# Two norm changes in a two-layer decoder on eight cores: squares folded on VectorE ahead of the sum matmul, and mixer norms moved ahead in program order

## The chip, the cores and the metric

One Trainium2 chip; the kernel runs on all 8 of its cores. Each core computes one prompt sequence of 2048 tokens and 16 sample sequences of 8 tokens; nothing is exchanged between cores. The metric is the device time of the slowest core, in microseconds (us). Some executions are slow: a die (cores 0 to 3 or 4 to 7) then shows a lower granted clock.

## The reference, cut to what matters

```python
def rmsnorm(x, g):
    y = x * rsqrt(mean(x * x, axis=-1) + EPS)
    return y * g

for i in range(2):                               # layers; D_MODEL 1024, D_FF 4096
    a = rmsnorm(h, norm_mix[i])                  # "mixer norm"
    u, bg, cg, v = split(a @ w_in[i])            # 4 x 512 columns
    y_pool = pool(u) * pool_scale[i]             # trailing-window means, then a 128x128 map per group
    y_conv = bg * conv3(cg * v)
    h = h + concat(y_pool, y_conv) @ w_out[i]
    m = rmsnorm(h, norm_mlp[i])
    h = h + relu(m @ w_up[i]) ** 2 @ w_down[i]
    gate = sigmoid(rmsnorm(h, norm_ple[i]) @ w_ple_gate[i])
    h = h + gate * (p[i] @ w_ple_proj[i])        # "gated stage"
return rmsnorm(h, norm_f), ...                   # "final norm", and the pool and conv states
```

There are seven norms over all tokens: three in each layer and the final one.

## The kernel before

The kernel holds h in SBUF with channels on partitions (8 blocks of 128) and tokens along the row, in five tiles of 512, 512, 512, 384 and 256 tokens. So a norm must sum squares across partitions. TensorE does that with an all-ones weight, once per block, adding up in PSUM:

```python
def norm(t, gbase, dst, dstB, halves=False):
    ...
        for hf in range(2):
            items = []
            for k in range(4 * hf, 4 * hf + 4):
                ...                                        # q: one of 4 square buffers
                P.op("act", ... activation(out=sq[:, q, 0:cn], in_=h[:, k, o:o + cn], func=AF.Square) ...)
                items.append((ones[:], sq[:, q, 0:cn], [onesB, sqB[q]]))
            ps = P.mm(items, cn, ps=ps, last=(hf == 1))    # 2 x 4 matmuls
        P.op("act", ... activation(out=rstd..., in_=ps..., func=AF.Ln, ...), kind="ln")
        P.op("act", ... activation(out=rstd..., in_=rstd..., func=AF.Exp, scale=-0.5), kind="ln")
        for k in range(KT):                                # 8 normalized blocks on VectorE
            P.op("dve", ... scalar_tensor_tensor(out=dst(k)..., in0=h[:, k, ...], scalar=gamma, in1=rstd...) ...)

def mixer_in(l, t, w):
    norm(t, V_NMIX + l * 8, ...)        # the norm of tile t stands right ahead of its matmuls
    ...                                 # 4 pool groups, then 4 conv groups
```

A list scheduler turns this program order into one fixed instruction stream per engine before the kernel is built. TensorE may draw operations from a window of 40 in program order.

Ln and Exp need one ScalarE table set (`kind="ln"`), the gated stage's Sigmoid another. Squares, copies and Relu run in either: of the 27 table loads in the trace before, 26 stand at the lines of Ln, Exp and Sigmoid, and one at a first Ln that the program issues at its start.

## Time and profile before

| | before |
|---|---|
| time, median of the first 5 runs | 1560.6 us |
| spans of the cores, profiled run | 1555.3 to 1558.5 us |
| matmuls that sum squares | 288 |
| ScalarE table loads | 27 |
| TensorE, VectorE, ScalarE busy | 98%, 57%, 34% |

The prediction below shows the page's lines and says how to read them. In all views PE is TensorE, PEld its weight loads, DVE VectorE, ACT ScalarE, POOL GpSimd and SP SyncE; L with a number is a line of that run's kernel.

### The profile page before, as it was taken

The numbers are of one execution on the slowest core, as the hardware profiler recorded it, in microseconds if no ns is written. First come the engines' busy times: TensorE is split into PE (matmuls) and PEld (weight loads), VectorE is DVE, ScalarE is ACT, GpSimd is POOL, SyncE is SP. The second block draws the span as 40 slices with busy tenths as digits, with TensorE's granted clock in tenths as the row PEclk, the third lists the DMA queues.
The fourth block names the chain that finished last, engine by engine and source line by source line (L and its number), as shares of the span: only waits on it lengthen the run. The fifth ranks groups of instructions, "written<-read, shape, count | busy, mean of one in ns | idle before, by whom it ended". The sixth has DMA issues, their size and how long they took to land.

```text
span 1558.5 us, 25041 instructions; the slowest of 8 cores (1555.3 to 1558.5 us)
## 1 busy us (share of the span) xinstructions
PE 1526.1 (98%) x8284; PEld 807.8 (52%) x8284; DVE 889.9 (57%) x1668; ACT 522.5 (34%) x1012; POOL 64.7 (4%) x122
## 2 busy tenths in 40 slices
PE   7999999999999999999989999999999999999997
PEld 4444565555555555454534446555555555554544
DVE  5758875444444444477677787744444444445778
ACT  4344453103103103335343444530230230233676
POOL 3000010000000000000000001000000000000000
PEclk9999999999999999999999999999999999999998
DMA  8900083421221221103230003722221221200024
GB/s 187 230 1 0 1 135 55 69 41 29 40 41 28 41 41 28 28 8 55 33 66 1 1 1 54 132 30 52 41 41 28 41 39 30 41 1 1 1 80 166
DMA packets 26062, 75.67 MB, mean 49 GB/s; under 512 B 2512, under 2 KB 7376, under 8 KB 25904
## 3 DMA queue, kind: packets, MB, share of 16 engines
q0 software_dynamic: 17600, 60.69, 22.8%
q1 hardware_dynamic: 8192, 13.31, 2.5%
q8 instruction: 71, 1.16, 0.3%
q14 instruction: 55, 0.45, 0.1%
q10 hardware_dynamic: 144, 0.05, 0.0%
HBM read 118.28 MB, written 10.10 MB: 82 GB/s over the span
## 4 chain that ended last, share of the span: by engine, by line
PE 91%; DVE 4%; DMA 2%; issue 1%; ACT 1%; POOL 0%; DVEq 0%; SPq 0%; ACTq 0%; POOLq 0%
PE ps L361 91%; DVE arena L576 2%; DMA poolw<-pool_w 1%; DVE h L720 1%; DVE arena L644 1%; DMA h<-x 1%; DVE h L576 0%; ACT sq L565 0%; DVE arena L652 0%; ACT arena L627 0%; ACT rstd L573 0%; ACT rstd L571 0%; POOL ring L529 0%; DVE arena L706 0%; DVE h L770 0%
## 5 line engine op out<-in xcount | busy, mean ns | idle before, releaser
L361 PE MATMUL ps<-arena,ring 128*128 128x512 bf16 (+2 forms) x7840 | 1464.9, 348 | 6.8 <-DVE arena L576 6.0
L361 PEld LDWEIGHTS ps<-arena,ring 128*128 128x128 bf16 x7840 | 767.0, 98 | 685.1 <-issue 19.3
L720 DVE TENSOR_TENSOR h<-h,ps 128x512 f32<-128x512 f32 (+2 forms) x400 | 241.6, 607 | 273.7 <-PE ps L361 273.3
L735 ACT ACTIVATE arena<-ps 128x512 f32<-128x512 f32 (+2 forms) x320 | 170.6, 533 | 640.5 <-PE ps L361 623.2
L736 DVE TENSOR_TENSOR arena<-arena 128x512 bf16<-128x512 f32 (+2 forms) x320 | 195.5, 612 | 268.1 <-ACT arena L735 267.9
L565 ACT ACTIVATE sq<-h 128x512 bf16<-128x512 f32 (+2 forms) x288 | 142.2, 546 | 133.3 <-PE ps L361 70.9
L576 DVE SCALAR_TENSOR_TENSOR arena<-h,vec,rstd 128x512 bf16<-128x512 f32 (+2 forms) x248 | 148.3, 654 | 26.7 <-ACT rstd L573 26.5
L361 PE MATMUL ps<-sq,ones 128*128 128x512 bf16 (+2 forms) x288 | 69.5, 351 | 11.1 <-ACT sq L565 10.1
L644 DVE TENSOR_TENSOR arena<-arena 128x526 f32<-128x526 f32 (+8 forms) x100 | 67.2, 672 | 6.9 <-ACT arena L627 4.3
L768 DVE TENSOR_TENSOR arena<-arena,ps 128x512 f32<-128x512 f32 (+2 forms) x80 | 47.4, 605 | 33.7 <-ACT arena L766 29.0
L706 DVE SCALAR_TENSOR_TENSOR arena<-arena,vec 128x512 f32<-128x512 f32 (+2 forms) x80 | 53.9, 676 | 19.5 <-ACT arena L702 15.9
L766 ACT ACTIVATE arena<-ps 128x512 f32<-128x512 f32 (+2 forms) x80 | 41.3, 532 | 49.9 <-PE ps L361 44.2
L361 PEld LDWEIGHTS ps<-sq,ones 128*128 128x128 bf16 x288 | 28.1, 98 | 43.1 <-issue 20.8
L770 DVE TENSOR_TENSOR h<-h,arena 128x512 f32<-128x512 f32 (+2 forms) x80 | 47.4, 610 | 4.6
L702 ACT ACTIVATE arena<-arena,vec 128x512 f32<-128x512 f32 (+2 forms) x40 | 30.1, 753 | 50.3 <-DVE arena L686 41.2
L627 ACT ACTIVATE arena<-ps 128x512 f32<-128x512 f32 (+2 forms) x48 | 22.7, 474 | 62.3 <-PE ps L361 51.0
L529 POOL DMA_DIRECT2D ring<-w_up x32 | 16.9, 530 | 615.8 <-PE ps L361 615.1
L686 DVE TENSOR_TENSOR arena<-arena,ps 128x512 f32<-128x512 f32 (+2 forms) x48 | 25.3, 530 | 15.9 <-PE ps L361 12.7
L681 ACT ACTIVATE arena<-ps 128x512 f32<-128x512 f32 (+2 forms) x48 | 22.3, 471 | 32.5 <-PE ps L361 28.9
L529 POOL DMA_DIRECT2D ring<-w_down x32 | 16.9, 529 | 324.0 <-PE ps L361 322.5
L664 ACT ACTIVATE arena<-ps,vec 128x512 bf16<-128x512 f32 (+2 forms) x40 | 24.8, 619 | 15.6 <-PE ps L361 15.6
L652 DVE SCALAR_TENSOR_TENSOR arena<-arena 128x512 bf16<-128x512 f32 (+2 forms) x48 | 25.7, 535 | 3.1 <-DVE carryE L631 0.4
(40 smaller groups left out, 230.3 us busy)
## 6 DMA issues: line engine op xcount, KB each, us to landing
ring<-w_up POOLq DMA_DIRECT2D x32, 512.0 KB, 6.3
ring<-w_down POOLq DMA_DIRECT2D x32, 512.0 KB, 6.5
ring<-w_in POOLq DMA_DIRECT2D x16, 512.0 KB, 9.5
y_t<-h SPq DMA_DIRECT2D x12, 512.0 KB, 2.8
h<-x POOLq DMA_DIRECT2D x4, 1024.0 KB, 29.2
ring<-w_out POOLq DMA_DIRECT2D x8, 512.0 KB, 25.5
ring<-w_gate POOLq DMA_DIRECT2D x8, 512.0 KB, 5.1
h<-x SPq DMA_DIRECT2D x4, 512.0 KB, 8.8
```

The lines of the kernel that those rows point to most:

```text
L361: return eng.matmul(self.psum[o.ps.bank][:, 0:o.width], lhsT=l, rhs=r, start=(o.first and j == 0), stop=(o.last and j == n - 1))
L529: o = P.dma("pool", lambda e, s=s, src=src: e.dma_start(out=ring[:, s, :], in_=src), 128 * 2048 * 4, f"ring{s}", writes=[ringB[s]], after= ...
L565: P.op("act", lambda e, q=q, k=k, o=o, cn=cn: e.activation(out=sq[:, q, 0:cn], in_=h[:, k, o:o + cn], func=AF.Square), c_act(cn), reads=[h ...
L576: P.op("dve", lambda e, n=n, k=k, o=o, c0=c0, cn=cn: e.scalar_tensor_tensor(out=dst(k)[:, c0:c0 + cn], in0=h[:, k, o:o + cn], scalar=vcol( ...
L644: P.op("dve", lambda e, to=to, src=src, v=v, sh=sh: e.tensor_tensor(out=af(to + v, ew - v), in0=af(src + v, ew - v), in1=af(src + v - sh, ...
L706: P.op("dve", lambda e, zo=zo, co=co, cwb=cwb, i=i: e.scalar_tensor_tensor(out=af(zo, zn), in0=af(co + i, zn), scalar=vcol(cwb + 4 * i), i ...
L720: P.op("dve", lambda e: e.tensor_tensor(out=h[:, c, toff:toff + tw], in0=h[:, c, toff:toff + tw], in1=ps.ap()[:, 0:tw], op=ALU.add), c_dve ...
L735: P.op("act", lambda e: e.activation(out=af(ro, tw), in_=ps.ap()[:, 0:tw], func=AF.Relu), c_act(tw), ps=[ps], writes=[rB])
L736: P.op("dve", lambda e: e.tensor_tensor(out=f_ap[t][c], in0=af(ro, tw), in1=af(ro, tw), op=ALU.mult), c_dve(tw), reads=[rB], writes=[fB[t] ...
L766: P.op("act", lambda e, ro=ro, p1=p1: e.activation(out=af(ro, tw), in_=p1.ap()[:, 0:tw], func=AF.Sigmoid), c_act(tw), ps=[p1], writes=[rB] ...
L768: P.op("dve", lambda e, ro=ro, p2=p2: e.tensor_tensor(out=af(ro, tw), in0=af(ro, tw), in1=p2.ap()[:, 0:tw], op=ALU.mult), c_dve(tw), ps=[p ...
L770: P.op("dve", lambda e, ro=ro, c=c: e.tensor_tensor(out=h[:, c, toff:toff + tw], in0=h[:, c, toff:toff + tw], in1=af(ro, tw), op=ALU.add), ...
```

## The change

The intent is to take norm sums off TensorE and to have the normalized blocks of the next mixer tile ready before TensorE needs them. The diff has five parts. The carry buffers' move into the arena (room for eight square blocks) is cut, as is the rest of the bookkeeping.

```diff
+        def first_norm():                       # layer 0, tile 0, in halves of 256; still 8 sum matmuls
+            ...
+                if i == 0:
+                    for o in P.ops[n0:]:
+                        o.lead = 4000.0         # schedule half 0 ahead of half 1's squares
+        def norm_stats(t, adds=True):
+            def add(a, b):                      # two blocks at once, bf16
+                P.op("dve", lambda e: e.tensor_tensor(out=sq[:, a:a + 2, 0:tw], in0=sq[:, a:a + 2, 0:tw], in1=sq[:, b:b + 2, 0:tw], op=ALU.add), ...)
+            for k in range(KT):
+                P.op("act", ... out=sq[:, k, 0:tw], in_=h[:, k, toff:toff + tw], func=AF.Square ...)
+                if adds and k % 4 == 3:
+                    add(k - 3, k - 1)
+            if adds:
+                add(0, 4)
+                P.op("dve", ... out=sq[:, 0, 0:tw], in0=sq[:, 0, 0:tw], in1=sq[:, 1, 0:tw], op=ALU.add ...)
+            ps = P.mm([(ones[:], sq[:, q, 0:tw], [onesB, sqB[q]]) for q in range(1 if adds else KT)], tw)
+            ...                                 # Ln, Exp
+        def norm_apply(t, n, gbase, dst, dstB): # the 8 normalizing instructions
 ...
         def mixer_in(l, t, w):
-            norm(t, V_NMIX + l * 8, lambda k: a[k][0], lambda k: aB[par][k], halves=(l == 0 and t == 0))
 ...                                             # pool half of tile t
+            if t + 1 < NT and (t > 0 or l == 0):
+                mix_apply(l, t + 1, norm_stats(t + 1))
 ...                                             # conv half of tile t
         def final(t):
-            norm(t, V_NF, lambda k: h[:, k, toff:toff + tw], lambda k: hB[k][t])
+            norm_apply(t, norm_stats(t, adds=t < 3), V_NF, lambda k: h[:, k, toff:toff + tw], lambda k: hB[k][t])
 ...
                 if l == DEPTH - 1:
                     final(t)
+                elif t == 1 or t == 3:          # in layer 0's gated stage: layer 1's first two mixer norms
+                    rs = norm_stats(t // 2)
+                elif t == 2 or t == 4:
+                    mix_apply(l + 1, t // 2 - 1, rs)
```

More of the change, by code (lines that the diff above doesn't have):

```diff
@@ L89, in __init__ @@
         self.fixed = None
+        self.lead = 0.0
 SEMLAT = 90.0
@@ L203, in schedule @@
                 a = min(a, ideal[o])
-            o.alap = a if o.fixed is None else -1e9 + o.fixed
+            o.alap = a - o.lead if o.fixed is None else -1e9 + o.fixed
         for o in ops:
@@ L409, in build @@
         arena = sb("arena", [128, AW], F32)
-        sq = sb("sq", [128, 4, 512], BF16)
+        sq = sb("sq", [128, KT, 512], BF16)
         rstd = sb("rstd", [128, 2, 512], F32)
@@ L415, in build @@
         invcnt = sb("invcnt", [128, 16], F32)
-        fix = sb("fix", [128, 16], F32)
-        carryE = sb("carryE", [128, 4, PB], F32)
-        carryC = sb("carryC", [128, 4, CB], F32)
         P.psum = [es.enter_context(nc.psum_tensor(f"ps{i}", [128, 512], F32)) for i in range(8)]
@@ L464, in build @@
         D_ = [take(256) for _ in range(2)]
+        CE_ = [take(PB) for _ in range(4)]
+        CC_ = [take(CB) for _ in range(4)]
         Z_ = [take(512), (M0 + 4 * W5, A.buf(M0 + 4 * W5, M0 + 4 * W5 + 512))]
@@ L469, in build @@
         SOUT = (T0, [A.buf(T0 + SO_P, T0 + SO_U), A.buf(T0 + SO_U, T0 + SO_C), A.buf(T0 + SO_C, T0 + SO)])
-        sqB = [Buf() for _ in range(4)]
+        SA = Arena()
+        sqB = [SA.buf(512 * k, 512 * k + 512) for k in range(KT)]
+        sqH = [[SA.buf(512 * k + 256 * i, 512 * k + 256 * i + 256) for i in range(2)] for k in range(KT)]
         rsB = [Buf() for _ in range(2)]
-        poolwB, vecB, onesB, invB, fixB = Buf(), Buf(), Buf(), Buf(), Buf()
-        ceB = [Buf() for _ in range(4)]
-        ccB = [Buf() for _ in range(4)]
+        poolwB, vecB, onesB, invB = Buf(), Buf(), Buf(), Buf()
+        fix, fixB = af(T0, 16), A.buf(T0, T0 + 16)
         ringB = [Buf() for _ in range(NSLOT)]
         halfB = [[Buf(), Buf()] for _ in range(NSLOT)]
-        st = dict(sq=0, rs=0, r=0, w=0)
+        st = dict(rs=0, r=0, w=0)
         def vcol(c):
@@ L551, in wk @@
             return ring[:, b.s, o:o + 128]
-        def norm(t, gbase, dst, dstB, halves=False):
-            toff, tw = TILES[t]
-            for i, (c0, cn) in enumerate([(0, 256), (256, 256)] if halves else [(0, tw)]):
-                hb = (lambda k: hH[k][i]) if halves else (lambda k: hB[k][t])
-                ab_ = (lambda k: aH[k][i]) if halves else dstB
-                o = toff + c0
-                ps = None
-                for hf in range(2):
-                    items = []
-                    for k in range(4 * hf, 4 * hf + 4):
-                        q = st["sq"]
-                        st["sq"] = (q + 1) % 4
-                        P.op("act", lambda e, q=q, k=k, o=o, cn=cn: e.activation(out=sq[:, q, 0:cn], in_=h[:, k, o:o + cn], func=AF.Square),
-                             c_act(cn), reads=[hb(k)], writes=[sqB[q]])
-                        items.append((ones[:], sq[:, q, 0:cn], [onesB, sqB[q]]))
-                    ps = P.mm(items, cn, ps=ps, last=(hf == 1))
-                n = st["rs"]
-                st["rs"] = 1 - n
-                P.op("act", lambda e, n=n, ps=ps, cn=cn: e.activation(out=rstd[:, n, 0:cn], in_=ps.ap()[:, 0:cn], func=AF.Ln, scale=1.0 / D, bias=EPS),
-                     c_act(cn), ps=[ps], writes=[rsB[n]], kind="ln")
-                P.op("act", lambda e, n=n, cn=cn: e.activation(out=rstd[:, n, 0:cn], in_=rstd[:, n, 0:cn], func=AF.Exp, scale=-0.5),
-                     c_act(cn), reads=[rsB[n]], writes=[rsB[n]], kind="ln")
-                for k in range(KT):
-                    P.op("dve", lambda e, n=n, k=k, o=o, c0=c0, cn=cn: e.scalar_tensor_tensor(
-                        out=dst(k)[:, c0:c0 + cn], in0=h[:, k, o:o + cn], scalar=vcol(gbase + k), in1=rstd[:, n, 0:cn],
-                        op0=ALU.mult, op1=ALU.mult), c_dve(cn, True), reads=[hb(k), rsB[n], vecB], writes=[ab_(k)])
@@ new lines, in rstd_of @@
+        def rstd_of(ps, n, tw):
+            P.op("act", lambda e: e.activation(out=rstd[:, n, 0:tw], in_=ps.ap()[:, 0:tw], func=AF.Ln, scale=1.0 / D, bias=EPS),
+                 c_act(tw), ps=[ps], writes=[rsB[n]], kind="ln")
+            P.op("act", lambda e: e.activation(out=rstd[:, n, 0:tw], in_=rstd[:, n, 0:tw], func=AF.Exp, scale=-0.5),
+                 c_act(tw), reads=[rsB[n]], writes=[rsB[n]], kind="ln")
+        def first_norm():
+            for i in range(2):
+                n0 = len(P.ops)
+                o = 256 * i
+                for k in range(KT):
+                    P.op("act", lambda e, k=k, o=o: e.activation(out=sq[:, k, o:o + 256], in_=h[:, k, o:o + 256], func=AF.Square),
+                         c_act(256), reads=[hH[k][i]], writes=[sqH[k][i]])
+                ps = P.mm([(ones[:], sq[:, k, o:o + 256], [onesB, sqH[k][i]]) for k in range(KT)], 256)
+                rstd_of(ps, i, 256)
+                for k in range(KT):
+                    P.op("dve", lambda e, i=i, k=k, o=o: e.scalar_tensor_tensor(
+                        out=ab(a_off[0] + k * 256, 512)[:, o:o + 256], in0=h[:, k, o:o + 256], scalar=vcol(V_NMIX + k), in1=rstd[:, i, 0:256],
+                        op0=ALU.mult, op1=ALU.mult), c_dve(256, True), reads=[hH[k][i], rsB[i], vecB], writes=[aH[k][i]])
+                if i == 0:
+                    for o in P.ops[n0:]:
+                        o.lead = 4000.0
@@ new lines, in norm_stats @@
+        def norm_stats(t, adds=True):
+            toff, tw = TILES[t]
+            def add(a, b):
+                P.op("dve", lambda e: e.tensor_tensor(out=sq[:, a:a + 2, 0:tw], in0=sq[:, a:a + 2, 0:tw], in1=sq[:, b:b + 2, 0:tw], op=ALU.add),
+                     75.0 + 1.042 * tw, reads=sqB[a:a + 2] + sqB[b:b + 2], writes=sqB[a:a + 2])
+            for k in range(KT):
+                P.op("act", lambda e, k=k: e.activation(out=sq[:, k, 0:tw], in_=h[:, k, toff:toff + tw], func=AF.Square),
+                     c_act(tw), reads=[hB[k][t]], writes=[sqB[k]])
+                if adds and k % 4 == 3:
+                    add(k - 3, k - 1)
+            if adds:
+                add(0, 4)
+                P.op("dve", lambda e: e.tensor_tensor(out=sq[:, 0, 0:tw], in0=sq[:, 0, 0:tw], in1=sq[:, 1, 0:tw], op=ALU.add),
+                     75.0 + 0.521 * tw, reads=sqB[0:2], writes=sqB[0:1])
+            ps = P.mm([(ones[:], sq[:, q, 0:tw], [onesB, sqB[q]]) for q in range(1 if adds else KT)], tw)
+            n = st["rs"]
+            st["rs"] = 1 - n
+            rstd_of(ps, n, tw)
+            return n
@@ new lines, in norm_apply, with norm @@
+        def norm_apply(t, n, gbase, dst, dstB):
+            toff, tw = TILES[t]
+            for k in range(KT):
+                P.op("dve", lambda e, k=k: e.scalar_tensor_tensor(out=dst(k), in0=h[:, k, toff:toff + tw], scalar=vcol(gbase + k),
+                                                                  in1=rstd[:, n, 0:tw], op0=ALU.mult, op1=ALU.mult),
+                     c_dve(tw, True), reads=[hB[k][t], rsB[n], vecB], writes=[dstB(k)])
+        def norm(t, gbase, dst, dstB):
+            norm_apply(t, norm_stats(t), gbase, dst, dstB)
@@ L580, in group, with mix_apply @@
+        def mix_apply(l, t, n):
+            par = t % 2
+            norm_apply(t, n, V_NMIX + l * 8, lambda k: ab(a_off[par] + k * 256, TILES[t][1]), lambda k: aB[par][k])
         def group(w, c, rhs, tw):
@@ L618, in mixer_in @@
                 else:
-                    P.op("dve", lambda e, eo=eo, g=g: e.tensor_copy(out=af(eo, PB), in_=carryE[:, g, :]), 80.0,
-                         reads=[ceB[g]], writes=[eB])
+                    P.op("dve", lambda e, eo=eo, g=g: e.tensor_copy(out=af(eo, PB), in_=af(CE_[g][0], PB)), 80.0,
+                         reads=[CE_[g][1]], writes=[eB])
                 if t == LT:
@@ L630, in mixer_in @@
                 if t < LT:
-                    P.op("dve", lambda e, eo=eo, g=g: e.tensor_copy(out=carryE[:, g, :], in_=af(eo + tw, PB)), 80.0,
-                         reads=[eB], writes=[ceB[g]])
+                    P.op("dve", lambda e, eo=eo, g=g: e.tensor_copy(out=af(CE_[g][0], PB), in_=af(eo + tw, PB)), 80.0,
+                         reads=[eB], writes=[CE_[g][1]])
                 else:
@@ L672, in mixer_in @@
                 else:
-                    P.op("dve", lambda e, co=co, j=j: e.tensor_copy(out=af(co, CB), in_=carryC[:, j, :]), 70.0,
-                         reads=[ccB[j]], writes=[cB])
+                    P.op("dve", lambda e, co=co, j=j: e.tensor_copy(out=af(co, CB), in_=af(CC_[j][0], CB)), 70.0,
+                         reads=[CC_[j][1]], writes=[cB])
                 if t == LT:
@@ L689, in mixer_in @@
                 if t < LT:
-                    P.op("dve", lambda e, co=co, j=j: e.tensor_copy(out=carryC[:, j, :], in_=af(co + tw, CB)), 70.0,
-                         reads=[cB], writes=[ccB[j]])
+                    P.op("dve", lambda e, co=co, j=j: e.tensor_copy(out=af(CC_[j][0], CB), in_=af(co + tw, CB)), 70.0,
+                         reads=[cB], writes=[CC_[j][1]])
                 else:
@@ L788, in build @@
                 w.setdefault(name, []).append(get())
+            if l == 0:
+                first_norm()
             mixer_in(l, 0, w)
```

## The prediction

> **What bounds the kernel now.** I read four views in this order: the list of cores (no die is slow: 1555.3 to 1558.5 us, clocks 0.991 to 0.994), the page, the groups by shape, and the table of stretches with the timeline around every place where TensorE stops.
>
> The page: TensorE is busy in 98% of the span, the chain that ended last lies on it for 91%, and the other engines are far from full on average. So time comes off only by taking matmuls away or by closing the gaps between them. The second row of groups is the target: 288 matmuls that only sum squares for the RMS norms (all-ones weights times the squared activations).
>
> ```profile
> PE 1526.1 (98%) x8284; PEld 807.8 (52%) x8284; DVE 889.9 (57%) x1668; ACT 522.5 (34%) x1012; POOL 64.7 (4%) x122
> ...
> PE 91%; DVE 4%; DMA 2%; issue 1%; ACT 1%; POOL 0%; DVEq 0%; SPq 0%; ACTq 0%; POOLq 0%
> ...
> L361 PE MATMUL ps<-sq,ones 128*128 128x512 bf16 (+2 forms) x288 | 69.5, 351 | 11.1 <-ACT sq L565 10.1
> ```
>
> Busy time is no cost here: 160 of these with 512 columns show a mean of 380 to 390 ns but overlap. The pace is what one more matmul costs, and the TensorE timeline gives it in unbroken runs:
>
> ```profile
> 38.45 13.98 PE L361 MATMUL ps<-arena,ring 128*128 128x512 bf16 x64
> ...
> 937.50 9.26 PE L361 MATMUL ps<-arena,ring 128*128 128x384 bf16 x56
> ...
> 1539.72 5.84 PE L361 MATMUL ps<-arena,ring 128*128 128x256 bf16 x52
> ```
>
> Taking off the last matmul's own 0.379, 0.324 and 0.269 us: 13.60/63 = 0.216, 8.94/55 = 0.1625, 5.57/51 = 0.109 us for 512, 384 and 256 columns. The span then splits like this. Real matmuls (4728, 1576 and 1576 of the three widths): 1021.2 + 256.1 + 172 = 1449 us. Norm sums after the first norm (160, 56, 56): 34.6 + 9.1 + 6.1 = 50. Start to the first real matmul: 19.8. Last matmul to the end: 9. Together 1528; the missing 30 us are stops and half-clock stretches.
>
> Where they lie (distances between matmul starts beyond the pace): 20 to 30 us 2.8, 53 to 62 us 4.0, 110 to 120 us 1.6, 170 to 210 us 3.2, 777 to 790 us 9.0, 870 to 890 us 2.0, 930 to 970 us 2.3, the last ten us of TensorE 3.3, and some 2 scattered. The table of stretches shows three of them; its columns are time and count on PE, PEld, DVE, ACT, POOL, then clock, DMA share, GB/s:
>
> ```profile
> 53.00:75.00 22.00, 20.57 (x85) 8.39 (x83) 18.98 (x37) 7.91 (x13) 0.00 (x0) 0.92 0.94 239
> ...
> 117.50:162.60 45.10, 43.62 (x202) 19.44 (x200) 38.12 (x73) 19.30 (x36) 0.00 (x0) 1.00 0.00 1
> ...
> 777.00:789.00 12.00, 6.48 (x20) 1.72 (x18) 6.25 (x12) 9.23 (x16) 1.06 (x2) 0.80 1.02 176
> 789.00:1000.00 211.00, 207.75 (x1102) 107.38 (x1102) 164.44 (x348) 93.54 (x196) 6.87 (x13) 1.00 0.18 30
> ```
>
> In 53 to 75, 85 matmuls at 0.216 would need 18.4 of the 22 us. In 777 to 789, the seam of the layers, only 20 matmuls run, and the clock falls. What TensorE waits for in a mixer is one normalized block at a time; VectorE makes one in (5.39 - 0.75)/7 = 0.66 us, TensorE uses it in 0.216. At the seam it is squares, the table load, Ln, Exp and then the blocks:
>
> ```profile
> 119.12 0.38 PE L361 MATMUL ps<-arena,ring 128*128 128x512 bf16 x1 [0.29 <-DVE arena L576]
> ...
> 781.21 1.28 ACT L571 ACT_TABLE_LOAD   x1 [0.60 <-PE ps L361]
> 782.51 0.60 ACT L571 ACTIVATE rstd<-ps 128x512 f32<-128x512 f32 x1
> ...
> 783.52 0.62 ACT L573 ACTIVATE rstd<-rstd 128x512 f32<-128x512 f32 x1
> ...
> 784.24 5.39 DVE L576 SCALAR_TENSOR_TENSOR arena<-h,vec,rstd 128x512 bf16<-128x512 f32 x8 [5.40 <-ACT rstd L573]
> ```
>
> **What the Trainium skill says.** "TensorE: Matmul & The Clock Gate", Wait — 56ns, not 53.3ns?: warm matmuls start N/2.4 GHz plus about 2.5 ns apart, 215.7 ns at 512 columns; the trace has 216, 162.5 and 109, so it agrees. The same page, What's actually happening: after an idle window of about 3.4 us the array runs at half clock. The trace agrees: mean clock 0.80 in the seam, 0.92 in 53 to 75. So closing a gap also takes back a slow stretch behind it. "VectorE: DVE Perf Modes", The perf-mode tier table: `tensor_tensor` on bf16 in SBUF makes two elements a cycle, on fp32 or from PSUM one. No all-bf16 add is in this trace, so this is untested here; the fp32 adds (0.69 us for 512 elements) agree with one. "Perfetto Trace Analysis", Optimizing Scalar/DVE Operations: each VectorE instruction on SBUF pays some 60 ns beyond its elements, about what the repeat distance of 0.61 us for 512 fp32 elements shows.
>
> **The change, part by part.**
>
> 1. Sums of squares. For 32 of the 35 tile norms, four VectorE adds fold the eight bf16 square blocks into one (three over two blocks, one over one), and one matmul replaces eight. Layer 0's first norm and the final norm of the last two tiles keep eight. The built instruction streams have 30, 14 and 20 such matmuls at 256, 384 and 512 columns, so 42, 42 and 140 go: 42 x 0.109 + 42 x 0.1625 + 140 x 0.216 = 4.6 + 6.8 + 30.2 = 41.6 us. All of it is TensorE time in stages that TensorE bounds, hence on the path.
>
> 2. VectorE's bill. At two elements a cycle the 1024-element add takes 0.53 + 0.08 = 0.62 us (estimate, rate from the DVE page, overhead from the trace), the last one 0.35: 2.2 us a 512-column norm, about 1.7 and 1.3 at 384 and 256. 20 + 6 + 6 norms: 44 + 10 + 8 = 62 us, so VectorE goes from 890 to about 950 of 1505 us, 63%. Beside TensorE in the MLP stages (VectorE 41 to 47% busy); not surely in the mixers. From 75 to 162.6 us VectorE does 26.6 + 38.1 = 64.7 us while TensorE issues 400 matmuls; a 512-column mixer tile (212 matmuls) is so 34.3 us of VectorE. After: 34.3 + 4.4 = 38.7 against 198 x 0.216 = 42.8 us of TensorE: 90%. Tight, but under.
>
> 3. Mixer norms earlier. The norm of tile t+1 now stands between the pool and conv halves of tile t, and layer 1's first two norms stand inside layer 0's gated stage (summed after tiles 1 and 3, applied after 2 and 4). So the blocks exist when TensorE arrives. In the built order 32 real matmuls for tile 1 follow tile 0's without a norm between, and at the seam the u-groups of layer 1 directly follow the last gate groups. The gated stage has room: VectorE 49.8 of 72 us, plus two norms (4.4 + 10.6) = 65. Two further table-load pairs there, 5.1 us of ScalarE, have room too (30 of 72).
> Expected: seam 9.0 to 0.5; 53 to 62 us 4.0 to 0.
>
> 4. Layer-0 start. Half 0's Ln and Exp no longer queue behind half 1's squares. Yet the chain of waits runs through the pool-weight load until 29.4 us, which nothing changes; only that 40 instead of 32 real matmuls precede it in the order. Gain at most 8 x 0.216 = 1.7 us.
>
> 5. Carry buffers and the small fix tile move into the arena to make room for eight square blocks: no cost that I find.
>
> Sum of stops afterwards: start 1.1; layer-0 mixers 4 (of 4.8 besides the closed gap: those at 110 and 170 to 210 shrink, VectorE at 90% makes others); seam 0.5; layer-1 mixers 3 (of 4.3); end 4.8, as VectorE has 6.6 us of adds more in a final stage where it was busy 62.7 of 80.5 us and TensorE now leaves 4.5 us earlier; scattered 2.5. That is 16 instead of 30. Time: 1560.6 - 41.6 - 14.5 = 1504 us, 3.6% less.
>
> **Rivals.** (a) VectorE becomes the mixers' bound. For it: 84% busy in 117 to 162 us already with stops, the adds are a dependent chain, and TensorE, which takes its instructions in order, now blocks at the sum matmul if the adds are late. Against it: 90% by count and TensorE has other groups ahead of each sum in the order. If so, 8 to 10 us more per layer: 1515 to 1525. (b) The adds run at one element a cycle: 1.15 instead of 0.62 us, 1.9 us a norm, a 512-column mixer tile then 42.5 of 42.8 us of VectorE; with stalls 1520 to 1530. The dense bf16 layout speaks against it. (c) Only the matmuls count, and the seam's wait moves elsewhere (ScalarE's extra tables delay the gated stage): 1560.6 - 41.6 + 2, about 1520. Layer 1's gated stage does the same table switches now without stopping TensorE before 1539 us, which speaks against it. (d) All stops of the mixers vanish and the end gains in full: about 1495.
>
> **Range and chances.** 1504, most likely with a tail to the slow side from (a) and (c); 1494 to 1518 should hold it 8 times in 10. A gain below 2% needs more than 1529, that is the whole closing of gaps lost and ten us of new stalls: 4%. Slower by over 2% would need VectorE to add some 70 us: 1%.
>
> **What would show it.** Step 1: 64 sum matmuls, none missing elsewhere. Step 2: 1024-element adds of about 0.7 us as the profile counts them (0.62 apart); 1.2 us would be rival (b). VectorE busy near 950. Step 3: no drop of the clock at the seam and no single matmuls waiting on the normalizing line after the pool-weight wait. Rival (a) would show TensorE idle before the sum matmuls or mixer matmuls, released by VectorE, over 8 us a layer. The prediction is wrong if TensorE's stops after the change do not fall below 20 us, or fall under 8.

## More of the kernel before

One more view is needed later: what happens once TensorE's last layer matmul has been issued. The table of stretches has time, then busy time and count on PE, PEld, DVE, ACT and POOL, then clock, DMA share and GB/s:

```profile
1538.00:1545.60 7.60, 7.51 (x66) 6.25 (x65) 7.49 (x18) 7.27 (x17) 0.00 (x0) 1.00 0.44 162
1545.60:1558.50 12.90, 1.80 (x8) 0.51 (x5) 9.45 (x22) 4.50 (x10) 0.00 (x0) 0.62 0.66 233
```

Three engines are full in the first row. In the second, TensorE has only norm sums left and VectorE works 9.45 of 12.9 us on 22 instructions. Then the last outputs are written.

The list scheduler lets TensorE draw operations from a window of 40 in program order.

Every other engine takes, of what is ready, the operation with the earliest latest-start time:

```python
pick = min((o for o in cs if ready[o] <= tau + 1.0), key=lambda o: (o.alap, o.i))
```

## The result, and the profile after

The changed kernel takes 1508.3 us (median of nine timed runs, 1508.1 over the fast ones) against 1561.0 us before: ratio 0.9666, 95% interval 0.9656 to 0.9676. Ratios here are the mean time of one kernel's fast runs over that of the other's in the same rounds, so they are not quite the ratio of the medians quoted. Executions in which one die ran at a lower clock are left out of the means. All runs gave correct results.

The page of the changed kernel, with the lines that answer to the prediction's first fence. The third is the group that sums squares:

```profile
PE 1477.9 (98%) x8062; PEld 784.6 (52%) x8062; DVE 934.1 (62%) x1796; ACT 536.9 (36%) x1020; POOL 64.7 (4%) x122
...
PE 93%; DVE 2%; DMA 2%; issue 1%; ACT 1%; POOL 0%; DVEq 0%; SPq 0%; ACTq 0%; POOLq 0%
...
L362 PE MATMUL ps<-sq,ones 128*128 128x256 bf16 (+2 forms) x64 | 19.0, 324 | 7.0 <-ACT sq L585 4.7
```

64 sum matmuls are left of 288, and VectorE's share on the chain of waits fell from 4% to 2%. TensorE's busy share is the same 98%: the kernel is still bound where it was, with less to do. The groups by shape give the price of one add over two blocks:

```profile
L581 DVE TENSOR_TENSOR sq<-sq 128x1024 bf16<-128x1024 bf16 x60 | 41.3, 690 | 12.8 <-ACT sq L585 12.5
```

690 ns for 1024 bf16 elements; the fp32 adds of 512 elements before the change took 687 ns with one input in PSUM (line 720 of the kernel before) and 689 with both in SBUF (line 770). Where adds queue up without a pause, the next instruction starts 0.60 us after either kind. So bf16 adds make twice the elements per unit of time, as the prediction assumed.

The stretches answer to those of the prediction: the first row is in layer 0's mixer, the next is the seam of the layers, and the last two are the end.

```profile
143.00:175.00 32.00, 32.00 (x177) 17.32 (x178) 30.00 (x74) 15.16 (x32) 0.00 (x0) 1.00 0.00 1
755.00:764.00 9.00, 9.00 (x44) 4.07 (x42) 9.00 (x22) 2.38 (x5) 1.06 (x2) 1.00 1.05 160
...
1481.70:1487.60 5.90, 5.83 (x50) 4.75 (x50) 5.56 (x13) 5.84 (x12) 0.00 (x0) 1.00 0.19 66
1487.60:1505.50 17.90, 2.15 (x8) 0.61 (x6) 12.74 (x29) 7.55 (x14) 0.00 (x0) 0.59 0.69 244
```

In the mixer VectorE is busy 30 of 32 us (94%) and TensorE has no gap at all. At the seam both are full and the clock is 1.00, where before 20 matmuls ran in 12 us at 0.80. At the end the opposite: 17.9 us after TensorE's last layer matmul instead of 12.9, with 12.74 us of VectorE instead of 9.45.

What TensorE still waits for (view of waits: us in total, times, longest):

```profile
PE ps L362 <- ACT sq L585: 4.7, 2, 3.8
PE ps L362 <- DVE arena L684: 2.3, 5, 0.6
PE ps L362 <- DMA ring<-w_in: 1.8, 1, 1.8
PE ps L362 <- DMA poolw<-pool_w: 1.6, 1, 1.6
```

Normalized blocks, 6.0 us in 14 waits in the same view before, are gone from the head of this list. The 4.7 us are squares of the last tile's final norm, at the end; the two DMA waits are at the start.

**Where the time went.** In both traces every layer matmul can be numbered (7880 of them), so the time at which a given matmul starts can be compared between the kernels. Taking off the sum matmuls that were removed (224 of them, at the pace of the prediction) leaves what the gaps gave. On core 7, the slowest of both profiles (1558.5 and 1505.5 us), measured from start to start of these matmuls:

| part | predicted gain, us | measured gain, us |
|---|---|---|
| 224 sum matmuls at TensorE's pace | 41.6 | 41.6 (counted, at the pace) |
| start, to matmul 131 | 1.7 | -1.0 |
| tile 0's end to tile 1 (matmuls 131 to 163) | 4.0 | 3.3 |
| other layer-0 mixers | 0.8 | 3.3 |
| seam of the layers | 8.5 | 8.7 |
| layer-1 mixers | 1.3 | 2.7 |
| scattered | -0.5 | -0.8 |
| after the last layer matmul | -1.5 | -5.0 |
| sum | 55.9 | 52.8 (spans: 53.0) |

The start differs from core to core: matmul 131 comes anywhere from 48.5 to 53.7 us in the changed kernel. Of the 5.0 us at the end, 2.4 are the last output write, which on this core lands 5.2 us after VectorE's last instruction instead of 2.8 (more on this below).

### The profile page after: what moved, and what is told of

The parts are those of the page before. It is cut to its first block, busy times and chain, and to the rows that moved or that the text cites. A ratio compares the mean times of both kernels' runs of the same rounds, so it can differ in the third digit from the quotient of the medians.

```text
span 1505.5 us, 24293 instructions; the slowest of 8 cores (1500.7 to 1505.5 us)
## 1 busy us (share of the span) xinstructions
PE 1477.9 (98%) x8062; PEld 784.6 (52%) x8062; DVE 934.1 (62%) x1796; ACT 536.9 (36%) x1020; POOL 64.7 (4%) x122
## 4 chain that ended last, share of the span: by engine, by line
PE 93%; DVE 2%; DMA 2%; issue 1%; ACT 1%; POOL 0%; DVEq 0%; SPq 0%; ACTq 0%; POOLq 0%
PE ps L362 93%; DMA ring<-w_in 1%; DMA h<-x 1%; DVE arena L676 0%; DVE h L602 0%; DVE arena L684 0%; ACT sq L585 0%; POOL ring L530 0%; ACT arena L800 0%; ACT L800 0%; DVE arena L746 0%; DVE arena L720 0%; DVE arena L740 0%; ACT arena L659 0%; POOL h L506 0%
## 5 line engine op out<-in xcount | busy, mean ns | idle before, releaser
L585 ACT ACTIVATE sq<-h 128x512 bf16<-128x512 f32 (+2 forms) x272 | 146.3, 561 | 148.7 <-DVE h L754 109.9
L602 DVE SCALAR_TENSOR_TENSOR arena<-h,vec,rstd 128x512 bf16<-128x512 f32 (+2 forms) x232 | 144.3, 666 | 4.2 <-ACT rstd L557 4.0
L581 DVE TENSOR_TENSOR sq<-sq 128x1024 bf16<-128x1024 bf16 (+2 forms) x96 | 58.7, 614 | 15.1 <-ACT sq L585 14.2
L530 POOL DMA_DIRECT2D ring<-w_up x32 | 16.9, 529 | 572.9 <-PE ps L362 572.0
L530 POOL DMA_DIRECT2D ring<-w_down x32 | 16.9, 529 | 321.3 <-PE ps L362 319.3
L362 PE MATMUL ps<-sq,ones 128*128 128x256 bf16 (+2 forms) x64 | 19.0, 324 | 7.0 <-ACT sq L585 4.7
```

What stands on the lines that cost most here:

```text
L362: return eng.matmul(self.psum[o.ps.bank][:, 0:o.width], lhsT=l, rhs=r, start=(o.first and j == 0), stop=(o.last and j == n - 1))
L581: P.op("dve", lambda e: e.tensor_tensor(out=sq[:, a:a + 2, 0:tw], in0=sq[:, a:a + 2, 0:tw], in1=sq[:, b:b + 2, 0:tw], op=ALU.add), 75.0 + ...
L585: P.op("act", lambda e, k=k: e.activation(out=sq[:, k, 0:tw], in_=h[:, k, toff:toff + tw], func=AF.Square), c_act(tw), reads=[hB[k][t]], w ...
L602: P.op("dve", lambda e, k=k: e.scalar_tensor_tensor(out=dst(k), in0=h[:, k, toff:toff + tw], scalar=vcol(gbase + k), in1=rstd[:, n, 0:tw], ...
```

## The experiments

Twelve runs. "Theory" is that of the prediction, or the one stated. The kernel before ran in the same calls, with medians over its fast runs of 1561.2, 1560.2 and 1560.7 us; the changed kernel was run again in the second call.

| run | edit to the changed kernel | fast median, us | ratio to before, 95% |
|---|---|---|---|
| r_after_again | none | 1508.4 | 0.9667 (0.9653 to 0.9680) |
| e1_sums_only | mixer norms back in their old places | 1527.7 | 0.9784 (0.9768 to 0.9800) |
| e2_moves_only | no adds, 8 sum matmuls everywhere | 1544.4 | 0.9893 (0.9877 to 0.9910) |
| e3_no_seam | layer 1's first mixer norms back after the seam | 1516.6 | 0.9715 (0.9699 to 0.9731) |
| e4_double_adds | every add made twice | 1513.5 | 0.9694 (0.9678 to 0.9711) |
| e5_ln_exp | Exp right behind its Ln, all norms | 1506.5 | 0.9653 (0.9640 to 0.9667) |
| e6_final_no_adds | no adds in the final norm | 1510.8 | 0.9681 (0.9668 to 0.9694) |
| e7_dma_order | second tile's x, later chunk, one weight block later | 1507.6 | 0.9661 (0.9648 to 0.9675) |
| e8_no_lead | first norm's early scheduling off | 1507.7 | 0.9663 (0.9649 to 0.9677) |
| e10_x1_later | all of the second tile's x two weight blocks later | 1508.5 | 0.9666 (0.9653 to 0.9680) |
| e11_pair_final | Exp right behind its Ln, final norms only | 1504.3 | 0.9641 (0.9627 to 0.9654) |
| e12_pair_final_x1 | e10 and e11 together | 1505.3 | 0.9646 (0.9632 to 0.9659) |

Several runs fell outside the band that the theory of their expectation gave: on the slow side e1 (by 0.7 us), e5 (0.5), e7 (0.7), e10 (1.5) and e12 (0.3), on the fast side e2 (0.6), e3 (0.4) and e11 (0.2).

One caution holds for all: the streams are made by a scheduler, so each edit also reorders instructions elsewhere.

### Each half of the change alone

```diff
# e1: sums only
         def mixer_in(l, t, w):
+            if l > 0 or t > 0:
+                mix_apply(l, t, norm_stats(t))
 ...
-            if t + 1 < NT and (t > 0 or l == 0):
-                mix_apply(l, t + 1, norm_stats(t + 1))
 ...
-                elif t == 1 or t == 3: ...
-                elif t == 2 or t == 4: ...
# e2: moves only
         def norm_stats(t, adds=True):
+            adds = False
```

> Only the sums of squares are folded on VectorE; every mixer norm stands where it stood before the change (at the start of its own tile, and layer 1's first norm after the seam). Theory (sums and stops are separate gains): the 224 removed matmuls give their 41.6 us, the stops at the first tile and the seam stay, and those of the mixers may grow by a few us, because the adds lengthen the chain from the last square to the first normalized block: 1517 to 1527 us, the seam losing 9 to 12 us as before. Rival (the chain of adds is on the path wherever a norm is waited for): about 3 us more for each of the ten waited-for mixer norms, so 1535 to 1550 us.

> Only the places of the norms change; every norm keeps its eight matmuls. Theory: the seam's 9 us and the first tile's 3 to 4 us come off, little else: 1560 minus 12 to 16 us, 1545 to 1549 us. Together with the run that only folds the sums the two gains should add up to the whole change's 53 us within 5 us. Rival (the early norms only pay because VectorE's fold frees TensorE or the other way round): the two gains add up to under 40 or over 65 us.

The sums alone gave 33.5 us of their 41.6 (fast medians; the verdict against a 2% gain stayed unclear, as the interval ends at it). The moves alone gave 16.8. Together 50.3, against 52.9 for the whole change (1561.0 less 1508.1), so the two halves nearly add up. In e1, TensorE still waits for these, and one stretch of layer 0's mixer looks full on VectorE:

```profile
PE ps L362 <- DVE arena L602: 7.2, 10, 4.3
...
PE ps L362 <- DVE sq L591: 2.4, 4, 1.1
```

```profile
110.00:160.00 50.00, 47.27 (x224) 22.05 (x227) 47.97 (x95) 23.26 (x46) 0.00 (x0) 1.00 0.00 1
```

Line 602 makes the normalized blocks and line 591 is the last add; the longest of these waits, 4.3 us, is the seam. Numbering the matmuls as in the table above (means of the six cores whose records are complete) shows where e1 lost what its matmul count promises: 2.5 us at the start, 2.3 in layer 1's mixers and 3.5 after the last layer matmul. In layer 0's mixers it lost nothing against the kernel before (0.1 us gained), although VectorE is busy 48 of 50 us there and TensorE stands 2.7. So rival (a) of the prediction, VectorE as the mixers' bound at 8 to 10 us per layer, does not appear here either; at most the 2.3 us in layer 1 are its share. In e2 layer 1's mixers gain 3.6 us, in the whole change 2.7.

### The seam

```diff
         def mixer_in(l, t, w):
+            if l > 0 and t == 0:
+                mix_apply(l, t, norm_stats(t))
 ...
-            if t + 1 < NT and (t > 0 or l == 0):
+            if t + 1 < NT:
 ...
-                elif t == 1 or t == 3: ...
-                elif t == 2 or t == 4: ...
```

> The whole change except that layer 1's first two mixer norms go back behind the seam (the first at the start of layer 1, the second between the halves of its first tile). Theory: the seam's stop returns, squares, adds, matmul, table load, Ln, Exp and the first blocks on the path, so 9 to 13 us slower than the changed kernel: 1517 to 1521 us, with the granted clock falling at the seam. The gated stage of layer 0 loses its two extra pairs of table loads. Rival (the seam's wait is hidden by the last gate groups of the small tile): under 4 us slower.

It is 8.2 us slower than the rerun of the changed kernel and 8.5 slower than its first fast median. That is a little under the expected band, and the stop is back in the TensorE timeline, with the low clock around it in the table of stretches:

```profile
756.08 0.38 PE L362 MATMUL ps<-sq,ones 128*128 128x512 bf16 x1
760.70 9.67 PE L362 MATMUL ps<-arena,ring 128*128 128x512 bf16 x21 [4.24 <-DVE arena L602]
```

```profile
750.00:768.00 18.00, 13.30 (x73) 7.28 (x71) 14.59 (x29) 8.47 (x17) 2.65 (x5) 0.75 0.91 149
```

After a stop of 4.24 us, 21 matmuls take 9.67 us where the pace needs 4.7 (20 x 0.216 + 0.38). Of these 5.0 us more, some 3 are still waiting: the first eight matmuls start 0.66 us apart, as fast as VectorE makes the blocks (5.38 us for eight). The rest, about 2 us, is the half clock, which shows in the next eight, 0.43 us apart. Thus the seam is worth about 8.5 us, most of it waiting for the norm and about a fifth the slow clock behind it. The prediction's 8.5 for this step stands.

### Is VectorE near to being the bound?

```diff
             def add(a, b):
                 P.op("dve", ... out=sq[:, a:a + 2, 0:tw] ...)
+                P.op("dve", ... out=sq[:, b:b + 2, 0:tw], in0=sq[:, a:a + 2, 0:tw], in1=sq[:, b:b + 2, 0:tw], op=ALU.add ...)
 ...                                     # and likewise a second one behind the last add, into block 1
```

The extra adds write blocks that are not read again, so results stay right.

> The changed kernel with every folding add done twice (the second into a block that is dead by then; the result stays right), so VectorE gets some 60 us more work and, where norms stand in the mixers, 4.4 us more per 512-column tile: 38.7 + 4.4 = 43.1 against TensorE's 42.8 us. Theory (VectorE is close to but under TensorE's time in the mixers, and free elsewhere): the mixers become VectorE's, 5 to 15 us slower than the changed kernel, with new TensorE stops released by VectorE in the mixers only. Rival A (VectorE is already the bound there): the doubling costs nearly all of what it adds in mixers and the final stage, 30 us or more. Rival B (ample slack): under 3 us.

VectorE's busy time rose from 934 to 985 us and the time by 5.4 us. In the mixer stretch that was 94% full it is now 99% full, and TensorE hardly notices:

```profile
143.00:175.00 32.00, 31.78 (x178) 17.02 (x176) 31.80 (x80) 15.99 (x36) 0.00 (x0) 1.00 0.01 1
```

3.8 of the 5.4 us are after the last layer matmul: from there to the end this kernel takes 21.0 us (mean of cores), the changed one 17.2. Layer 1's mixers lost 1.2 us more than in the changed kernel, layer 0's 0.3. So the time falls into the band of the theory by luck: it asked for new stops in the mixers, and most of the loss is at the end. The adds are nearly free wherever TensorE has other work ahead of the sum matmul in its stream, and cost at the very end.

### The start: what sets it

```diff
# e8
-                        o.lead = 4000.0
+                        o.lead = 0.0
# e7: {weight blocks loaded: x chunks that follow}
-        FIRST = {2: [(1, 0)], 3: [(1, 4)], 8: ...
+        FIRST = {2: [(1, 0)], 4: [(1, 4)], 8: ...
# e10
-        FIRST = {2: [(1, 0)], 3: [(1, 4)], 8: ...
+        FIRST = {4: [(1, 0)], 5: [(1, 4)], 8: ...
```

> The changed kernel, with one load moved: the second half of tile 1's activations is loaded after the fifth weight block instead of after the fourth. In the changed kernel TensorE starts 3.3 us earlier than before, then waits 1.8 us for the fifth block until 36.9 us, runs the next 16 matmuls at half clock and has lost the whole lead by the 96th. Theory (the start is bound by the order of the loads): the fifth block lands some 3.5 us earlier, the wait and the slow stretch go, 1.5 to 3.5 us faster. Rival (the loads' total bandwidth binds, or tile 1's norm then comes late): within 1 us, the wait turning up at a later block or at tile 1's first blocks.

> The changed kernel without the preference for the first half of the first norm. On the mean of the cores the changed kernel issues its first real matmul 2.8 us earlier than before, and the 96th at the same time as before. Theory (the loads bind the start): within 1 us of the changed kernel although the first real matmul comes some 2 us later. Rival (the early start is worth what the prediction gave it): 1.5 to 2 us slower.

> The changed kernel with both halves of tile 1's activations moved back in the queue of loads: behind the fifth and the sixth weight block (from behind the third and the fourth). Moving the second half alone gained nothing: the wait went from the fifth block to the sixth, 2.07 us. Theory (the loads bind by what has to be there by when): the pool weights and the fourth to sixth block land some 3 to 6 us earlier, the waits go, and the 132nd real matmul comes 2 to 3 us earlier: 1505.5 to 1507 us. Rival (total bandwidth binds, as the eighth block is needed then anyway and tile 1's norm comes later): within 1 us.

None moved the time: their fast medians lie within 0.8 us of the rerun's, and the intervals overlap. The first layer matmul comes at 19.3 us before, 16.5 after and 18.5 in e8 (means of the six cores with complete records). Yet matmul 131 starts at 51.4 before, 51.3 after, 52.6 in e7, 52.3 in e8 and 51.7 in e10, closer together than the cores of one run. The TensorE timeline of the changed kernel shows the two waits that eat the early start:

```profile
28.06 0.59 PE L362 MATMUL ps<-arena,poolw 128*128 128x512 bf16 x2 [1.65 <-DMA poolw<-pool_w]
...
36.87 5.29 PE L362 MATMUL ps<-arena,ring 128*128 128x512 bf16 x16 [1.77 <-DMA ring<-w_in]
```

In e7 and in e10 the wait is for a later block, one line from each:

```profile
42.75 2.84 PE L362 MATMUL ps<-arena,ring 128*128 128x512 bf16 x8 [2.07 <-DMA ring<-w_in]
```

```profile
45.42 2.98 PE L362 MATMUL ps<-arena,ring 128*128 128x512 bf16 x8 [2.68 <-DMA ring<-w_in]
```

So the change's early first norm is worth nothing here. Whichever transfer is put off, TensorE waits for the one that comes last: three orders end at the same place. Whether fewer bytes in the first 50 us would help was not tried.

### The end: why it grew

> The changed kernel once more, on this call's chip, as the mark for the three that follow: ratio 0.966 to 0.967.

The rerun confirms the time, and the longer end: 17.4 us from the last layer matmul to the end of the span (mean of cores), 17.2 in the first profile, 13.3 before. Two explanations compete. Either the adds that the final norm still has for its first three tiles load VectorE when it is full, or the order on ScalarE is at fault. The groups of before and after have table loads in Exp's own line:

```profile
L573 ACT ACT_TABLE_LOAD x6 | 7.7, 1283 | 0.1
```

```profile
L557 ACT ACT_TABLE_LOAD x8 | 10.3, 1283 | 0.1
```

They should not exist, as Ln has just loaded that table. They mean that a Sigmoid slipped in between. The number of loads can't explain the longer end: all lines together have 35 instead of 27, but the eight more belong to the two norms that were moved into layer 0's gated stage. Layer 1's gated stage has 20 in both kernels, five of them in Exp's line, and e1 and e3, without those two, have 27 in all and the changed kernel's end (table below). What did change there is when Exp comes. The ScalarE timelines show it for the third tile's final norm, first in the kernel before:

```profile
1526.46 0.60 ACT L571 ACTIVATE rstd<-ps 128x512 f32<-128x512 f32 x1
...
1532.97 0.63 ACT L573 ACTIVATE rstd<-rstd 128x512 f32<-128x512 f32 x1
```

Exp starts 5.9 us after Ln is done, still 12.3 us ahead of TensorE's last layer matmul. In the changed kernel:

```profile
1473.41 1.28 ACT L555 ACT_TABLE_LOAD   x1
1474.70 0.60 ACT L555 ACTIVATE rstd<-ps 128x512 f32<-128x512 f32 x1
1475.32 1.28 ACT L800 ACT_TABLE_LOAD   x1
...
1482.19 1.28 ACT L557 ACT_TABLE_LOAD   x1
1483.49 0.63 ACT L557 ACTIVATE rstd<-rstd 128x512 f32<-128x512 f32 x1
1484.03 0.47 ACT L555 ACTIVATE rstd<-ps 128x384 f32<-128x384 f32 x1
1484.52 1.28 ACT L800 ACT_TABLE_LOAD   x1
```

Exp starts 8.2 us after Ln is done, and only 3.8 us ahead of the last layer matmul. VectorE can't normalize the tile in the meantime. Its timeline shows that this work comes late: four of the tile's 512-column blocks run after TensorE's last layer matmul, which starts at 1487.3 (one at 1488.54, not shown, and three in the row of 1489.53; a merged row shows the shape of its first instruction):

```profile
1484.22 2.74 DVE L602 SCALAR_TENSOR_TENSOR h<-h,vec,rstd 128x512 f32<-128x512 f32 x4
...
1489.53 2.61 DVE L602 SCALAR_TENSOR_TENSOR h<-h,vec,rstd 128x512 f32<-128x512 f32 x4
...
1493.38 6.96 DVE L602 SCALAR_TENSOR_TENSOR h<-h,vec,rstd 128x384 f32<-128x384 f32 x15
```

From 1486.88 us on it never pauses. Three experiments tell the explanations apart: e5 keeps every Exp right behind its Ln, e11 does so in the final norms only, e6 takes the adds out of the final norm.

```diff
# e5, and e11 with the pair set in final() only
+                    if e == "act" and hold is not None and hold in cs:
+                        pick = hold
+                        tau = max(free[e], ready[hold])
 ...
+            if e == "act":
+                hold = o.pair                   # set on Ln: its Exp
# e6
-            norm_apply(t, norm_stats(t, adds=t < 3), V_NF, ...)
+            norm_apply(t, norm_stats(t, adds=False), V_NF, ...)
```

> The changed kernel, with one rule added to the scheduler: ScalarE does each norm's Exp right behind its Ln. In the changed kernel a Sigmoid slips between them in the gated stages, so each norm there pays four table loads (1.28 us each) instead of two; 35 loads in all, 8 more than before the change. Theory (ScalarE's table loads set the last 25 us, where TensorE gets ahead of it): 10 to 14 loads fewer, and the end gains 2 to 5 us: 1503.5 to 1506 us. Rival (the end is set by VectorE, 94% busy from 1443 to 1487 us, whatever ScalarE does): under 1 us.

> The changed kernel, with the final norms of all tiles summed by eight matmuls (the change folds those of the first three tiles). VectorE loses 6.6 us of adds in the last 75 us, TensorE gets 21 matmuls of 512 columns back, 4.5 us. Theory (table loads on ScalarE set the end): the last real matmul 4 us later, the end about 1 to 3 us later than in the changed kernel, as the time that TensorE spends comes out of its lead over ScalarE. Rival (VectorE's adds made the end 5 us longer): the end gets shorter by more than TensorE's 4.5 us, so the kernel is equal or up to 2 us faster.

> The changed kernel with Exp kept right behind Ln in the five final norms only. With that rule on all norms the tail after the last real matmul fell from 17.4 to 13.7 us (mean of the cores) and table loads from 35 to 21, but 2 us were lost at the seam, where early normalizing blocks went ahead of the gate's work on VectorE. Theory: only the tail's part remains, 2.5 to 4 us faster than the changed kernel: 1504.5 to 1506 us. Rival (the gain of the first run came from the gated stage, not from the tail): under 1 us.

> Both last edits together, as the version that should beat both kernels. Theory: the start and the end are independent, the gains of the two runs add up to within 1 us: 1501.5 to 1505 us, ratio to the kernel before 0.962 to 0.9645. Rival: not additive, no better than the better of the two.

I counted VectorE's instructions that start after TensorE's last layer matmul (means of the eight cores):

| kernel | last layer matmul starts, us | VectorE instructions after it (normalizing) | their busy time, us | to VectorE's last instruction, us | to the end, us |
|---|---|---|---|---|---|
| before | 1543.9 | 22 (16) | 9.8 | 10.4 | 13.3 |
| changed | 1486.7 | 28 (20) | 13.0 | 13.0 | 17.2 |
| e6, no adds in the final norm | 1491.5 | 23 (16) | 10.1 | 12.6 | 15.5 |
| e2, no adds at all | 1525.7 | 23 (16) | 10.0 | 12.6 | 15.4 |
| e5, all pairs | 1488.3 | 24 (16) | 10.2 | 10.2 | 13.7 |
| e11, final pairs | 1486.5 | 24 (16) | 10.2 | 10.2 | 13.8 |
| e4, double adds | 1489.3 | 34 (27) | 17.4 | 17.4 | 21.0 |

The fifth column agrees on all cores of a run to 0.02 us, and it is 13.0 again in the rerun, e1, e3, e7, e8 and e10. The last column adds the landing of the last output write, 2.8 to 4.4 us later by run. That part follows no edit: e10 has the changed kernel's 13.0 us and 2.9 for the write, the rerun 4.4. So of the 4.0 us by which the end grew, 2.6 are VectorE's and 1.4 are the write's.

e11 took off 4.1 us against the rerun and 3.4 against e8, which has the changed kernel's end (16.9 us). It has 29 table loads, and in its ScalarE timeline Exp follows Ln at once:

```profile
1475.34 0.60 ACT L562 ACTIVATE rstd<-ps 128x512 f32<-128x512 f32 x1
1476.03 0.63 ACT L564 ACTIVATE rstd<-rstd 128x512 f32<-128x512 f32 x1
1476.68 1.28 ACT L809 ACT_TABLE_LOAD   x1
```

The four 512-column blocks are no longer left over, and VectorE is done 2.8 us sooner after the last layer matmul, as soon as in the kernel before. TensorE's last layer matmul stands where it stood (1486.5), so the gain is all in the end. Removing the adds (e6) makes VectorE's end only 0.4 us shorter, and TensorE then has 21 more sum matmuls and arrives 4.2 to 4.8 us later: 2.4 us lost on balance. The adds do have a share in the late Exp: with them the third tile's Ln starts 12.6 us ahead of the last layer matmul, without them (e6, e2) 18.5. But then the fourth tile's Exp comes 7.0 us after its Ln and 4.5 us behind the last layer matmul. So the adds pay even here, and what VectorE's end can get back is the late Exp.

e5 gained 1.9 us against the rerun, less than e11 although its end is as short. It loses at the seam, where between layer matmuls 3500 and 3939 it takes 81.1 us and the changed kernel 79.2. There TensorE stands for the gated stage's Sigmoid, by its timeline:

```profile
755.57 1.25 PE L369 MATMUL ps<-arena,ring 128*128 128x256 bf16 x10 [1.50 <-ACT arena L807]
```

With Exp early, VectorE takes the normalizing blocks of the next layer ahead of the gate's own work, and the gate falls behind. e12 adds e10's later load to e11 and gains nothing more, as the rival said. The start stays bound by its transfers.

**e11 is the best kernel:** 1504.3 us, ratio 0.9641 to the kernel before. Its advantage over the changed kernel is 0.2 to 0.3%, seen in two comparisons (e11 and e12 against e8 and e10: 3.4 and 3.1 us).

## Why the prediction was right, and where its sizes were off

The prediction said 1504 us in a range of 1494 to 1518; it came to 1508. By its own steps:

1. **Sums of squares.** 64 sum matmuls as said, and TensorE stayed the bound in the stages they were taken from. e1 shows that they alone bring 33.5 us. Of the other 8, 3.5 are the longer end, which the whole change has too, and the rest is at the start and in layer 1's mixers. Right.
2. **VectorE's bill.** 934 us busy where about 950 was expected; 690 ns for the large add where about 700 was expected. Rival (b), one element a cycle, is out. Rival (a) is out: VectorE reaches 94% in the mixer without stopping TensorE, and even 99% in e4; in e1, with the norms in their old places, it costs 2.3 us in one layer's mixers and none in the other's, where the rival had 8 to 10 in each.
3. **Mixer norms earlier.** The seam gave 8.7 of 8.5 us, and e3 confirms it. (For the clock there the prediction said that the trace agrees with an idle window of 3.4 us. The clock does fall, but TensorE's longest stop at the seam is 2.63 us on core 7.) The two norms moved into layer 0's gated stage cost eight table loads, 10.3 us of ScalarE, where it counted two pairs, 5.1 us; TensorE hardly stopped for it. The prediction left 4 and 3 us of stops in the two layers' mixers besides, out of 4.8 and 4.3; they gave back 3.3 and 2.7 us, some 4 us more than it assumed. It was too careful there.
4. **Layer-0 start.** It allowed at most 1.7 us and found none: the early first matmul waits for the weights again (e7, e8, e10). The mechanism that it named, the loads, is what binds; it should have booked zero.
5. **Carry buffers.** No cost found. No run tested this part alone.

The term of the sum that was mis-sized is the end: "end 4.8, as VectorE has 6.6 us of adds more in a final stage", a loss of 1.5 us in TensorE's last stops, with the 9 us from its last matmul to the end left as they were. On core 7 these stops grew by 2.6 us, and the time behind the last matmul to 11.4 us, 5.0 in all. On the mean of cores it is 4.0 us: VectorE's last instruction comes 2.6 us later after the last layer matmul, and the last write lands 1.4 us later, which stays unexplained. The prediction counted VectorE's work but not ScalarE's order. The reason it gave, the adds, does not suffice: without them VectorE's end is only 0.4 us shorter and the kernel is slower (e6), while keeping Exp behind Ln brings VectorE's end back to 10.2 us and the kernel gains 3.4 to 4.1 us (e11). Rival (c) had named ScalarE's tables, but in layer 0's gated stage, where the changed kernel's TensorE timeline shows one stop of 0.36 us.

Luck has a part in how near the number came. The mixers and the seam gave some 4 us more than predicted, tile 1, the start and the end some 7 less, and these errors partly cancel.

The prediction's own test asked for stops between 8 and 20 us. Counted as it did, as distances between matmul starts beyond the pace from the first layer matmul on, they fell from 30.9 to 20.5 us on core 7, and to 18.9 on core 7 of the rerun. So the test is missed by 0.5 us in one profile and met in the other: the result is at its edge. The sum behind its 16 had 1.1 us of stops at the start and 4.8 at the end; with TensorE starting 3.3 us earlier, core 7 has some 7 us of them at the start, and 5.9 behind the last layer matmul.

What stays open: in e11 VectorE is busy 17.7 of the 18.8 us ahead of TensorE's last layer matmul and without a pause behind it, so how much of the remaining 13.8 us a better order of VectorE's work could take was not measured. The last output writes land 2.8 to 4.4 us after VectorE's last instruction, by run, and why they differ was not pursued. The kernel before has late Exps too; what pairing them would give it was not tried.

## What to carry to other kernels

When an engine is busy 98% of the span, count the instructions that a change takes off it, at the pace they have in unbroken runs, and then look for who is late in each stage. Work given to a second engine was nearly free here where the first had other work queued ahead of the result, even at 94% to 99% of the second one, and cost time behind the first one's last layer matmul. And when the first engine gets faster, look at the order on the others: a scheduler that doesn't see ScalarE's table sets put a Sigmoid between Ln and Exp. It had done so before the change too, but afterwards the late Exp left four blocks to be normalized behind TensorE's last layer matmul, and undoing it gained 3 to 4 us.

## What the Trainium skill lacked or had wrong

- "ScalarE: Activation LUTs", What ACT_TABLE_LOAD costs: its 1283 ns for the load agree with every group above. It adds a drain of about 1380 ns, 2.66 us in total for a switch. The traces here show no such time: in the changed kernel Ln ends at 1475.30, the load starts at 1475.32, and the first Sigmoid starts at 1476.61, which makes 1.31 us from one function to the next. Sized by the page, the eight extra loads would count double.
- "TensorE: Matmul & The Clock Gate", What's actually happening: it gives the half clock after at least one idle window of about 3.4 us. The length of half-clock stretches agrees (3.41 us or a multiple of it inside the kernels). Read as the least length of one stop, the figure does not hold here: a much shorter stop can be enough, and a longer one need not be. In the changed kernel a wait of 1.77 us on core 7 was followed by 3.4 us at half clock (the row below), while core 0 of the same run waited 2.48 us at the same place and ran on at full clock.

```profile
36.87:40.29 3.42, 3.42 (x9) 1.19 (x10) 2.92 (x7) 1.88 (x4) 0.00 (x0) 0.50 1.03 168
```
